# Gated linear attention in a four-layer model: the heads' work as stages between the dense products

## The chip, the cores and the metric

One core of one Trainium2 chip runs the whole program: four layers over 512 tokens of width 1024, batch 1, all in float32. The metric is the device time of one execution in microseconds. Three runs of the kernel before gave a median of 2174.72 us (2171.09 to 2180.26).

## What is computed

Two layers of a first kind, then two of a second; the change touches the first kind alone. Such a layer normalises its input, multiplies it by a wide matrix and splits the result into the inputs of two branches: softmax attention from low-rank q and kv (MLA), and gated linear attention (GLA) with four heads, keys of 64 and values of 128, run forwards and backwards over the sequence. Both branches are gated, joined, projected and added to the residual. The GLA branch in one direction, in chunks of C = 64 tokens:

```python
log_a = log_sigmoid(lr @ w_gate + b_gate) / 16
b   = cumsum(log_a, within the chunk)
ref = b[C // 2 - 1]
A   = tril((q * exp(b - ref)) @ (k * exp(ref - b)).T)
o_intra = A @ v
o_inter = (q * exp(b)) @ state
state   = state * exp(b_last) + (k * exp(b_last - b)).T @ v
o = rmsnorm(o_fwd + o_bwd) * silu(gate)
```

## The kernel before, in words

Every dense product is made of three matmuls on rounded halves (`mm3`, L177 to L179): weights and activations are split into a high part `wh`, `xh` and a rest `wl`, `xl` of type float32r. Weights come as a stream of 128x1024 tiles: `take` (L138 to L142) transfers one on SP's queue into one of two raw buffers, ScalarE rounds it to `wh`, VectorE subtracts for `wl`; there are four buffers of each. `n_out` makes token-major results, four token tiles one after another, each over all eight k; `t_out` makes one feature-major tile of 128x512, from one weight tile.

`layer1` orders a layer so. `ev_kv` normalises and transposes the compressed kv, the rope key and, per token tile, the 32 rows `lrT` of the gates' low-rank input (L601 to L611; transposes use one PSUM bank, `tr`). Then gq and gk (`t_out` four times), gv and the compressed q (`n_out`), the MLA gate `do_ga` (`t_out` four times) and the GLA gate gg (`n_out`). Then `gla(h)` for four heads, then the products of w_uq and w_ukv (`do_qr`, `do_qn`, `do_kn`, `do_vm`), then softmax attention.

One `gla(h)` keeps the forward direction in partitions 0 to 63 and the backward one in 64 to 127. It does: the gate product z from 32 rows in plain float32 (L485); the softplus of it on ScalarE, with Exp and Ln; two scans on VectorE for the sums b; copies of q and k of the head into both halves by DMA on SP's queue (L509, L510); four exponentials (L517) and four products (L518); the scores of both directions into banks 4 and 5 (L531); two predicated copies into masks (L533) and their sum (L535); the transpose of the scaled keys; eight chunk products kv (L543), again into banks 4 and 5; the recurrence of S over the chunks, twelve steps on VectorE (L551, L557); then, per token tile, the own-chunk product (L564) and two products with the states before (L567) into bank 7; normalisation, the gate's factor, and transposes into the layer's output.

What sets the order: the tile framework lays out every engine's queue by a priority that follows program order, and lets a later instruction go first while an earlier one's inputs aren't expected to be ready. `high_priority(offset=n)` moves instructions up by n places. Each engine then runs its queue in order and waits where an input is late:

```python
with tc.high_priority(offset=300):
    for h in range(4):
        gla(h)
```

So the heads come in as soon as their inputs are expected, from the end of `do_ga` on. Weight tiles are moved up by `lead`, 15 or 20 places.

Of the kernel before, what the change touches and what calls it, by code (L numbers as in the profile page):

```python
# [8 lines left out]
F32 = mybir.dt.float32  # L9
# [8 lines left out]
P = 128  # L18
# [19 lines left out]
def shape_consts():  # L38
# [36 lines left out]
    cst1 = np.concatenate([np.broadcast_to(inv1, (P, 32)), scan], 1).astype(f)  # L75
    icst1 = np.concatenate([same & (i <= j), same & (i >= j)], 1).astype(np.int32)
# [12 lines left out]
def body(ctx, tc, a, out, plan, n1=LAYERS, n2=LAYERS, dbg=None):  # L89
# [116 lines left out]
    def n_out(w, xk, c, evac, k_outer=False):  # L206
# [159 lines left out]
    def block1():  # L366
        with ExitStack() as c1:
# [3 lines left out]
            cst1 = b1.tile([P, 32 + SEQ], F32, name="cst1")  # L371
            inv1, scan = cst1[:, 0:32], cst1[:, 32:32 + SEQ]
            icst1 = b1.tile([P, 256], I32, name="icst1")
# [56 lines left out]
            for l in range(n1):  # L430
                xt, xd, pss = layer1(l, xt, xd, CS, SN, scan, icst1, amask, pss)
# [10 lines left out]
    def layer1(l, xt, xd, CS, SN, scan, icst1, amask, pss):  # L442
        lead[0] = 15
        xk = klist(xt)
        with ExitStack() as cl:
# [23 lines left out]
            row, lrT, gate_w = early[:, 0:ROW1], early[0:32, 768:1280], early[:, 1280:1792]  # L469
            nc.sync.dma_start(row, a["row1"][l:l + 1, :].partition_broadcast(P))  # L470
            nc.sync.dma_start(gate_w, a["par1"][l][:, 4:PAR1])
            q_gain, kv_gain, o_gain = row[:, 0:384], row[:, 384:640], row[:, 640:768]
            gqk = pl.tile([P, 4, SEQ], F32, tag="gqk", name="gqk", bufs=1)
# [7 lines left out]
            nc.vector.tensor_scalar(nbias, par[:, 0:4], -1.0, None, ALU.mult)  # L481

            def gla(h):
                z = bank("z")
                nc.tensor.matmul(z, gate_w[0:32, tsl(h)], lrT, start=True, stop=True)  # L485
                bias = par[:, h:h + 1]
                b = gt("wa", 4)
                nc.scalar.activation(b, z, AF.Abs, bias=bias)
                nc.scalar.activation(b, b, AF.Exp, scale=-1.0)
                nc.scalar.activation(b, b, AF.Ln, bias=1.0)  # L490
                la = gt("wa", 4)
                nc.scalar.activation(la, z, AF.Relu, scale=-1.0, bias=nbias[:, h:h + 1])
                nc.vector.tensor_tensor(la, la, b, ALU.add)
# [3 lines left out]
                                             op0=ALU.mult, op1=ALU.add)  # L497
                bv = b.rearrange("p (n c) -> p n c", c=64)
                ref = sml.tile([P, 2, 8], F32, tag="ref", name="ref", bufs=2)
                nc.vector.tensor_copy(ref[F, 0], bv[F, :, 31])  # L500
                nc.vector.tensor_copy(ref[B, 0], bv[B, :, 32])
                nc.vector.tensor_copy(ref[F, 1], bv[F, :, 63])
                nc.vector.tensor_copy(ref[B, 1], bv[B, :, 0])
                dec = sml.tile([P, 8], F32, tag="dec", name="dec", bufs=2)
                nc.scalar.activation(dec, ref[:, 1], AF.Exp, scale=-1 / 16)
                hb = tsl(h % 2, 64)
                q2, k2 = gt("wm", 4), gt("wm", 4)
                for dst, src in ((q2, gq), (k2, gk)):
# [3 lines left out]
                def minus(i):  # L512
                    nc.vector.tensor_tensor(la.rearrange("p (n c) -> p n c", c=64), bv, end(ref[:, i], 64), ALU.subtract)

                def scaled(dst, src, e, s):
                    ex = gt("wa", 4)
                    nc.scalar.activation(ex, e, AF.Exp, scale=s)  # L517
                    nc.vector.tensor_tensor(dst, src, ex, ALU.mult)  # L518
# [878 lines left out]
```

## Time and profile before

| | us |
|---|---|
| median of three runs | 2174.72 |
| lowest, highest | 2171.09, 2180.26 |
| profiled execution, its time | 2182.32 |
| profiled execution, its span | 2180.5 |
| TensorE matmuls busy | 2084.5 |
| VectorE busy | 1271.3 |
| ScalarE busy | 969.2 |
| GpSimd (POOL) busy | 175.7 |

Times in the profile count from the span's start. The mixing stage of layer 0 lies at about 34 to 230 us and that of layer 1 at about 395 to 582; softmax attention follows each. Engines: PE is TensorE's matmuls, PEld its weight loads, DVE is VectorE, ACT is ScalarE. A busy PE is a modelled span of pipelined matmuls, so the distance from one start to the next tells more than a duration.

### The profile page before, as it was taken

Reading aid. Unit: us, or ns where it says so; the run is one execution under the profiler, and the core shown is the slowest. Engines: PE = TensorE matmul, PEld = TensorE weight load, DVE = VectorE, ACT = ScalarE, POOL = GpSimd, SP = SyncE. Lnnn points to the kernel's source line nnn. Section 1 sums busy time; section 2 is a strip of 40 time slices with the busy share of each in tenths; the row PEclk is TensorE's granted clock in tenths of the full one; section 3 lists DMA queues with packets and bytes.
Section 4 is the critical chain, followed back from the end, with each engine's and each line's share of the span. In section 5 each row is a group of like instructions: output and inputs, shape, how many; then the busy total and the mean of one; then the engine's idle time right before and its main releaser. Section 6 shows DMA issues by size and latency. Waiting matters only on the chain.

```text
span 2180.5 us, 28221 instructions
## 1 busy us (share of the span) xinstructions
PE 2084.5 (96%) x10832; PEld 1716.3 (79%) x10832; DVE 1271.3 (58%) x2120; ACT 969.2 (44%) x1819; POOL 175.7 (8%) x305
## 2 busy tenths in 40 slices
PE   7998999998999899999999999999999999999998
PEld 6866887876687788877788888878887778888886
DVE  6278745358855577574466524566757437662464
ACT  4275544355534463336444424446332645442342
POOL 1000000000000211110200000021112011000001
PEclk9999999999999999999999999999999999999999
DMA  5222133332122432121443333243311234333332
GB/s 172 79 73 66 58 108 113 114 109 70 42 97 91 159 113 77 52 64 39 145 152 98 95 96 98 90 129 114 92 54 33 70 116 148 97 98 95 98 98 94
DMA packets 73781, 207.47 MB, mean 95 GB/s; under 512 B 16560, under 2 KB 17584, under 8 KB 73392
## 3 DMA queue, kind: packets, MB, share of 16 engines
q1 hardware_dynamic: 62640, 200.96, 29.5%
q10 hardware_dynamic: 11008, 4.72, 0.9%
q8 instruction: 85, 1.39, 0.3%
q14 instruction: 48, 0.39, 0.1%
HBM read 182.32 MB, written 17.04 MB: 91 GB/s over the span
## 4 chain that ended last, share of the span: by engine, by line
PE 68%; issue 9%; DVE 7%; ACT 7%; DMA 6%; POOL 3%; SPq 0%; POOLq 0%; ACTq 0%; DVEq 0%
PE ps_mm L178 16%; PE ps_mm L179 16%; PE ps_mm L177 16%; DMA wr<-in_w 4%; DVE wl L142 2%; PE ps_o L1188 2%; ACT wh L141 2%; PE ps_tr L270 1%; PE ps_pt L270 1%; POOL rstd L277 1%; PE ps_mo L179 1%; PE ps_mo L177 1%; PE ps_mo L178 1%; PE ps_s L1171 1%; ACT xn L292 1%
## 5 line engine op out<-in xcount | busy, mean ns | idle before, releaser
L142 DVE TENSOR_TENSOR wl<-wr,wh 128x1024 fp32r<-128x1024 f32 (+4 forms) x304 | 360.3, 1188 | 426.3 <-ACT wh L141 422.7
L141 ACT CAST wh<-wr 128x1024 fp32r<-128x1024 f32 (+4 forms) x304 | 309.3, 1019 | 362.5 <-PE ps_mm L179 150.9
L177 PE MATMUL ps_mm<-wh,xh 128*128 128x512 f32 (+2 forms) x736 | 283.8, 387 | 3.3 <-ACT wh L141 3.2
L178 PE MATMUL ps_mm<-wl,xh 128*128 128x512 f32 (+2 forms) x736 | 283.6, 386 | 2.1 <-DVE wl L142 1.8
L179 PE MATMUL ps_mm<-x2h,wl 128*128 128x512 f32 (+1 forms) x768 | 285.5, 372 | 0.0
L177 PE MATMUL ps_mm<-x2h,wh 128*128 128x512 f32 (+1 forms) x768 | 285.4, 372 | 0.0
L178 PE MATMUL ps_mm<-x2l,wh 128*128 128x512 f32 (+1 forms) x768 | 285.4, 372 | 0.0
L179 PE MATMUL ps_mm<-wh,xl 128*128 128x512 f32 (+2 forms) x736 | 282.6, 385 | 0.0
L177 PEld LDWEIGHTS ps_mm<-wh,xh 128*128 128x128 f32 x736 | 140.5, 191 | 30.5 <-ACT wh L141 7.1
L177 PEld LDWEIGHTS ps_mm<-x2h,wh 128*128 128x128 f32 x768 | 144.7, 188 | 25.2
L179 PEld LDWEIGHTS ps_mm<-x2h,wl 128*128 128x128 f32 x768 | 144.7, 188 | 24.9
L178 PEld LDWEIGHTS ps_mm<-x2l,wh 128*128 128x128 f32 x768 | 144.7, 188 | 24.8
L178 PEld LDWEIGHTS ps_mm<-wl,xh 128*128 128x128 f32 x736 | 141.0, 192 | 29.0 <-DVE wl L142 6.0
L179 PEld LDWEIGHTS ps_mm<-wh,xl 128*128 128x128 f32 x736 | 141.0, 192 | 24.9 <-issue 2.2
L1282 DVE SCALAR_TENSOR_TENSOR rt<-ps_mm,par,rt 128x511 f32<-128x511 f32 (+1 forms) x176 | 131.3, 746 | 3.0
L177 PE MATMUL ps_mm<-xh,wh 128*128 128x512 f32 x320 | 127.4, 398 | 0.1
L179 PE MATMUL ps_mm<-xh,wl 128*128 128x512 f32 x320 | 127.4, 398 | 0.0
L178 PE MATMUL ps_mm<-xl,wh 128*128 128x512 f32 x320 | 127.3, 398 | 0.0
L293 POOL TENSOR_SCALAR r2h<-ss 128x1 f32<-128x1 f32 x48 | 18.7, 389 | 961.7 <-ACT th L292 758.8
L178 PE MATMUL ps_mm<-wl,hh 128*128 128x512 f32 x224 | 88.1, 395 | 0.8 <-DVE wl L142 0.8
L177 PE MATMUL ps_mm<-wh,hh 128*128 128x512 f32 x224 | 87.7, 393 | 0.5 <-ACT wh L141 0.4
L179 PE MATMUL ps_mm<-wh,hl 128*128 128x512 f32 x224 | 87.2, 391 | 0.0
(398 smaller groups left out, 3866.7 us busy)
## 6 DMA issues: line engine op xcount, KB each, us to landing
wr<-in_w SPq DMA_DIRECT2D x270, 512.0 KB, 3.6
gain<-in_gain SPq DMA_DIRECT2D x13, 512.0 KB, 6.1
wr<-in_w SPq DMA_DIRECT2D x14, 384.0 KB, 3.2
x<-in_x SPq DMA_DIRECT2D x8, 512.0 KB, 6.0
wm<-gqk SPq DMA_DIRECT2D x32, 128.0 KB, 2.5
xd<-x SPq DMA_DIRECT2D x8, 512.0 KB, 2.6
xs<-xd SPq DMA_DIRECT2D x8, 512.0 KB, 4.0
xs<-xm SPq DMA_DIRECT2D x8, 512.0 KB, 4.5
```

Of the source, the lines that this page charges most:

```text
L141: nc.scalar.copy(hi[:, :n], raw[:, :n])
L142: nc.vector.tensor_tensor(lo[:, :n], raw[:, :n], hi[:, :n].bitcast(F32), ALU.subtract)
L177: nc.tensor.matmul(ps, l[0], r[0], start=start, stop=False)
L178: nc.tensor.matmul(ps, l[0], r[1], start=False, stop=False)
L179: nc.tensor.matmul(ps, l[1], r[0], start=False, stop=stop)
L270: nc.tensor.transpose(ps[:w, tsl(j)], src[:, tsl(j, w)], ident)
L277: nc.gpsimd.tensor_tensor(r2[:, :w], r[:, :w], powm[:, :w], ALU.pow)
L292: nc.scalar.activation(junk[i], halves[i], AF.Square, accum_out=ss[:, i:i + 1])
L293: nc.gpsimd.tensor_scalar(r[:, i:i + 1], ss[:, i:i + 1], 1.0 / D, r[:, 0:1] if i else EPS, ALU.mult, ALU.add)
L1171: nc.tensor.matmul(o_s, q_[own], kl[own, h // 2, :w], start=False, stop=True)
L1188: nc.tensor.matmul(o[:, tsl(h, 64)], p_[:, tsl(i * (qt + 1) + j)], av[:, j, tsl(h, 64)], start=j == 0, stop=j == qt)
L1282: nc.vector.scalar_tensor_tensor(acc[:, j:], ps[:, :SEQ - j], par[:, w0 + 3 * m + 2 - j:w0 + 3 * m + 3 - j], acc[:, j:], ALU.mult, ALU.add)
```

## The change

The gate product takes 96 rows: the low-rank input transposed three times over (high part, high part, rest), against the weights' high part, rest and high part, in float32r. Within a chunk, q and k are scaled once, relative to the chunk's middle; the state is kept relative to the middle of its next chunk, so `dec` spans from middle to middle, the scores' keys serve for the chunk products as well, and q for the past is the scores' q times `dec`, on POOL. The forward scores are multiplied by a mask with 2 on the diagonal of each 64-block; the backward ones are copied over the strictly lower part. A head is cut into eight functions; `n_out` takes a dictionary `then` of what to trace after which token tile. gg now stands before the compressed q. The weighted output overwrites `sgg`. Buffers change: `wm` 4 to 5 (three tiles a head instead of four), `wb` 2 to 1, one `y`, three `gb`, and a tile `lgr` for the gate product's operands; `lrT` and the gate weights leave `early`.

```diff
-    def n_out(w, xk, c, evac, k_outer=False):
+    def n_out(w, xk, c, evac, k_outer=False, then={}):
...
             evac(t, ps)
+            if t in then:
+                then[t]()
...
+            lgr = pl.tile([P, 1024], F32R, name="lgr")
+            lrT, gate_w = lgr[0:96, 0:512], lgr[0:96, 512:1024]
+            nc.scalar.copy(gate_w, gate_raw)
+            nc.vector.tensor_tensor(gate_w[32:64], gate_raw[32:64], gate_w[32:64].bitcast(F32), ALU.subtract)
...
-                nc.tensor.matmul(z, gate_w[0:32, tsl(h)], lrT, start=True, stop=True)
+                nc.tensor.matmul(z, gate_w[:, tsl(h)], lrT, start=True, stop=True)
...
+                for hf, m, e in ((F, 31, 63), (B, 32, 0)):
+                    nc.vector.tensor_copy(ref[hf, 0], bv[hf, :, m])
+                    nc.vector.tensor_tensor(ref[hf, 1], bv[hf, :, e], bv[hf, :, m], ALU.subtract)
+                nc.gpsimd.memset(ref[:, 2], 0.0)
+                nc.gpsimd.tensor_tensor(ref[F, 2, 1:8], ref[F, 0, 1:8], ref[F, 1, 0:7], ALU.add)
+                nc.gpsimd.tensor_tensor(ref[B, 2, 0:7], ref[B, 0, 0:7], ref[B, 1, 1:8], ALU.add)
...
-                minus(0)
-                qi, ki = gt("wm", 4), gt("wm", 4)
-                scaled(qi, q2, la, -1 / 16)
-                scaled(ki, k2, la, 1 / 16)
-                scaled(q2, q2, b, -1 / 16)
-                minus(1)
-                scaled(k2, k2, la, 1 / 16)
+                for x, s in ((ki, 1 / 16), (qi, -1 / 16)):
+                    ex = gt("wa", 4)
+                    nc.scalar.activation(ex, la, AF.Exp, scale=s)
+                    nc.vector.tensor_tensor(x, x, ex, ALU.mult)
+                qe = gt("wm", 5)
+                nc.gpsimd.tensor_tensor(qe.rearrange("p (n c) -> p n c", c=64),
+                                        qi.rearrange("p (n c) -> p n c", c=64), end(dec, 64), ALU.mult)
...
-                for i in range(2):
-                    nc.vector.copy_predicated(amask[i], mid(icst1[:, tsl(i)], NT), v4(sc[i]))
-                A = gt("wb", 2)
-                nc.vector.tensor_tensor(v4(A), amask[0], amask[1], ALU.add)
+                A = amask[h % 2]
+                for u in range(2):
+                    rs = tsl(u, 64)
+                    nc.vector.tensor_tensor(A[rs, :, rs], v4(sf)[rs, :, rs], mid(diag2[rs], NT), ALU.mult)
+                nc.vector.copy_predicated(A, mid(icst1, NT), v4(sb))
...
+            def gla_own(h):
+                gs[h]["o"] = o = bank("og")
+                for t in range(NT):
+                    nc.tensor.matmul(o[:, tsl(t)], gs[h]["A"][:, t], gv[:, t, tsl(h)], start=t == 0, stop=False)
+            def gla_past(h):
+                o, qe, S = (gs[h][n] for n in ("o", "qe", "S"))
+                for n in range(8):
+                    nc.tensor.matmul(o[tsl(n % 2, 64), tsl(n // 2)], qe[:, tsl(n, 64)], S[:, n],
+                                     start=False, stop=n >= 6)
...
-                nc.tensor.transpose(pt[0:32, 384:512], rp[:, 64:96], ident)
+                nc.tensor.transpose(pt[0:96, 384:512], rp[:, 64:160], ident)
...
-                nc.vector.tensor_copy(lrT[:, tsl(t)], pt[0:32, 384:512])
+                nc.vector.tensor_copy(lrT[:, tsl(t)], pt[0:96, 384:512])
+                nc.vector.tensor_tensor(lrT[64:96, tsl(t)], pt[64:96, 384:512], lrT[64:96, tsl(t)].bitcast(F32),
+                                        ALU.subtract)
...
-            with tc.high_priority(offset=300):
-                for h in range(4):
-                    gla(h)
...
+            gla_gate(0)
+            gla_gate(1)
+            do_gqk(0)
+            gla_scale(0)
+            gla_gate(2)
+            do_gqk(1)
+            gla_scale(1)
+            n_out(take_n("w_in", l, rng(6), range(KT)), xk, 512,
+                  lambda t, ps: nc.scalar.copy(gv[:, t], ps), then={1: lambda: gla_scores(0), 2: lambda: gla_gate(3)})
+            n_out(take_n("w_in", l, rng(9), range(KT)), xk, 512, ev_gg, then={
+                0: lambda: (gla_state(0), gla_scale(2)), 1: lambda: gla_own(0),
+                2: lambda: (gla_scores(1), gla_past(0)), 3: lambda: gla_state(1)})
+            n_out(take_n("w_in", l, rng(0), range(KT)), xk, 384, ev_q, then={
+                0: lambda: (gla_norm(0), gla_scale(3)), 1: lambda: gla_own(1), 2: lambda: gla_scores(2),
+                3: lambda: gla_past(1)})
+            do_ga(0)
+            gla_state(2)
+            gla_norm(1)
+            do_ga(1)
+            gla_own(2)
+            gla_scores(3)
+            do_ga(2)
+            gla_past(2)
+            gla_state(3)
+            do_ga(3)
+            gla_norm(2)
...
+                         range(3)), cq, 256, ev_qr, then={1: lambda: gla_own(3), 3: lambda: gla_past(3)})
+            do_qn(0)
+            gla_norm(3)
+            do_qn(1)
+            gla_out(0)
             do_kn()
+            for h in (1, 2, 3):
+                gla_out(h)
             do_vm()
```

## Rows read from the trace of the kernel before

**Rows 1.** The page, engine totals: busy us (share of the span), instructions.
```profile
PE 2084.5 (96%) x10832; PEld 1716.3 (79%) x10832; DVE 1271.3 (58%) x2120; ACT 969.2 (44%) x1819; POOL 175.7 (8%) x305
```

**Rows 2.** Stretches: from:to, length, busy us of PE, PEld, DVE, ACT, POOL, granted clock, DMA.
```profile
34.00:110.00 76.00, 72.25 (x344) 61.46 (x343) 28.35 (x63) 26.21 (x51) 6.15 (x14) 0.98 0.30 97
110.00:230.00 120.00, 107.06 (x573) 78.00 (x573) 95.27 (x176) 71.94 (x150) 7.12 (x14) 0.91 0.26 72
170.00:230.00 60.00, 50.92 (x316) 37.51 (x315) 48.87 (x98) 30.02 (x80) 5.06 (x10) 0.91 0.28 77
460.00:582.00 122.00, 107.30 (x596) 79.08 (x595) 97.42 (x180) 72.88 (x151) 7.68 (x15) 0.96 0.26 78
520.00:582.00 62.00, 52.87 (x333) 39.11 (x332) 51.05 (x101) 31.65 (x83) 5.24 (x10) 0.94 0.25 75
```

**Rows 3.** Timeline of PE: start us, us, instruction [idle before <-releaser].
```profile
138.19 0.39 PE L178 MATMUL ps_mm<-wl,xh 128*128 128x512 f32 x1
138.42 0.39 PE L179 MATMUL ps_mm<-wh,xl 128*128 128x512 f32 x1
141.16 0.44 PE L567 MATMUL ps_og<-S,wm 128*64 128x128 f32 x4 [2.35 <-issue]
...
145.84 0.63 PE L178 MATMUL ps_mm<-wl,xh 128*128 128x512 f32 x1
146.27 0.63 PE L179 MATMUL ps_mm<-wh,xl 128*128 128x512 f32 x1
```

**Rows 4.** Groups of DVE in 110:230: count | busy us, mean ns | idle before.
```profile
L557 DVE SCALAR_TENSOR_TENSOR S<-S,dec,ps_kv 64x128 f32<-64x128 f32 x24 | 8.5, 354 | 0.8
L551 DVE SCALAR_TENSOR_TENSOR S<-S,dec,ps_kv 64x128 f32<-64x128 f32 x24 | 8.1, 339 | 0.8
```

**Rows 5.** Waits of PE in 110:232: us in total, times, longest.
```profile
PE ps_kv L543 <- ACT wb L539: 2.0, 1, 2.0
PE ps_mm L177 <- ACT th L658: 1.7, 1, 1.7
```

**Rows 6.** Timeline of PE around one gate product.
```profile
129.16 1.12 PE L485 MATMUL ps_z<-early 32*128 32x512 f32 x2 [0.15 <-ACT wa L492]
130.21 0.66 PE L270 MATMUL ps_ks<-ident,wm 128*128 128x128 f32 x4
130.62 0.48 PE L179 MATMUL ps_mm<-xh,wl 128*128 128x512 f32 x1
```

**Rows 7.** Timeline of PE in one head's output product, at full clock.
```profile
184.12 0.44 PE L567 MATMUL ps_og<-S,wm 128*64 128x128 f32 x4 [0.30 <-issue]
184.49 0.49 PE L564 MATMUL ps_og<-gv,wb 128*128 128x128 f32 x2
...
185.28 0.49 PE L564 MATMUL ps_og<-gv,wb 128*128 128x128 f32 x2
```

**Rows 8.** Groups of ACT and DVE in 110:230 (one layer).
```profile
L517 ACT ACTIVATE wa<-wa 128x512 f32<-128x512 f32 x16 | 9.8, 630 | 3.8 <-DVE wm L518 3.1 <-DVE wa L513 0.5
L518 DVE TENSOR_TENSOR wm<-wm,wa 128x512 f32<-128x512 f32 x16 | 10.8, 688 | 3.7 <-PE ps_og L567 3.5
```

**Rows 9.** Timeline of POOL and of DVE at 844 us, in the second block.
```profile
844.40 2.53 POOL L1063 TENSOR_TENSOR dt<-A,cst 128x512 f32<-128x512 f32 x2
844.46 1.24 DVE L1014 TENSOR_SCALAR cq<-rstd 128x4 f32<-128x4 f32 x1
```

**Rows 10.** Timeline of PE and of DVE, transposes of kv.
```profile
401.13 0.41 PE L270 MATMUL ps_tr<-ident,th 128*128 128x128 f32 x2 [0.92 <-DVE early L611]
40.66 0.28 DVE L611 COPY early<-ps_tr 32x128 f32<-32x128 f32 x1
```

**Rows 11.** Timeline of PE where the compressed q follows gv, layers 0 and 1.
```profile
86.53 0.62 PE L177 MATMUL ps_mm<-wh,xh 128*128 128x384 f32 x2 [1.66 <-ACT wh L141]
...
445.23 0.44 PE L178 MATMUL ps_mm<-wl,xh 128*128 128x384 f32 x1 [0.21 <-DVE wl L142]
```

**Rows 12.** Waits of SP's queue, whole span: us in total, times, longest.
```profile
SPq L509 <- PE ps_sb L531: 12.6, 4, 5.6
```

More of the change, by code (lines that the diff above doesn't have):

```diff
@@ L509, in gla @@
+                for dst, src in ((qi, gq), (ki, gk)):
                     nc.sync.dma_start(dst[F], src[h // 2][hb])
                     nc.sync.dma_start(dst[B], src[h // 2][hb])
[L512 to L515 removed]
+                la = gt("wa", 4)
+                nc.vector.tensor_tensor(la.rearrange("p (n c) -> p n c", c=64), bv, end(ref[:, 0], 64), ALU.subtract)
@@ L561, in gla @@
-                with tc.high_priority(offset=-20):
-                    o = bank("og")
-                    for t in range(NT):
-                        nc.tensor.matmul(o[:, tsl(t)], A[:, tsl(t)], gv[:, t, tsl(h)], start=True, stop=False)
-                        for u in range(2):
-                            n = 2 * t + u
-                            nc.tensor.matmul(o[tsl(u, 64), tsl(t)], q2[:, tsl(n, 64)], S[:, n], start=False, stop=True)
-                    y = gt("wb", 2)
-                    ss = sml.tile([P, 4], F32, tag="ss4", name="ss4")
-                    for t in range(NT):
-                        nc.scalar.activation(y[:, tsl(t)], o[:, tsl(t)], AF.Square, accum_out=ss[:, t:t + 1])
-                    r = rstd(ss, 4, 1.0 / P)
-                    for t in range(NT):
-                        nc.scalar.activation(y[:, tsl(t)], o[:, tsl(t)], AF.Copy, scale=r[:, t:t + 1])
-                    nc.vector.tensor_tensor(v4(y), v4(y), sgg[:, :, tsl(h)], ALU.mult)
-                    ps = flip(y, role="og")
-                    split(ps, yt[0][1][:, h], yt[1][1][:, h])
+                nc.scalar.copy(S[F, 1], kv[0][F, tsl(0)])
@@ new lines, in gla_state @@
+                nc.scalar.copy(S[B, 6], kv[1][B, tsl(3)])
+                for n in range(1, 7):
+                    m = 7 - n
+                    nc.vector.scalar_tensor_tensor(S[F, n + 1], S[F, n], dec[F, n:n + 1],
+                                                   kv[n % 2][F, tsl(n // 2)], ALU.mult, ALU.add)
+                    nc.vector.scalar_tensor_tensor(S[B, m - 1], S[B, m], dec[B, m:m + 1],
+                                                   kv[m % 2][B, tsl(m // 2)], ALU.mult, ALU.add)
@@ new lines, in gla_norm @@
+            def gla_norm(h):
+                o = gs[h]["o"]
+                y = gt("y", 1)
+                ss = sml.tile([P, 4], F32, tag="ss4", name="ss4")
+                for t in range(NT):
+                    nc.scalar.activation(y[:, tsl(t)], o[:, tsl(t)], AF.Square, accum_out=ss[:, t:t + 1])
+                r = rstd(ss, 4, 1.0 / P)
+                for t in range(NT):
+                    nc.scalar.activation(y[:, tsl(t)], o[:, tsl(t)], AF.Copy, scale=r[:, t:t + 1])
+                nc.vector.tensor_tensor(sgg[:, :, tsl(h)], v4(y), sgg[:, :, tsl(h)], ALU.mult)
@@ L579, in layer1, with gla_out @@
+            def gla_out(h):
+                ps = bank("og")
+                for t in range(NT):
+                    nc.tensor.transpose(ps[:, tsl(t)], sgg[:, t, tsl(h)], ident)
+                split(ps, yt[0][1][:, h], yt[1][1][:, h])
             ckh = pc.tile([P, 2, SEQ], F32R, name="ckh")
```

130 lines of the change are left out of this document (57 added, 73 removed).

## The prediction

> **What bounds the kernel now.** I read the page's engine totals first. TensorE's matmuls are busy for 96% of the span [rows 1], so time is won only where TensorE idles, runs below full clock, or issues less. Next I cut the span into stretches, each layer's mixing stage apart [rows 2]. Its dense first part (34 to 110 us) is nearly full on TensorE while VectorE works 28.35 of 76 us. The part with the heads is different: in layer 0 (110 to 230 us) TensorE is busy 107.06 of 120 us at a mean granted clock of 0.91, and in layer 1 (460 to 582 us) 107.30 of 122 at 0.96. Idle time is 12.9 + 14.7 = 27.6 us. Clock lost, (1 - 0.91) x 120 + (1 - 0.96) x 122, is 15.7 us at most, since part of the slow time is itself idle. Together 43.3 us: the whole pool of waiting that the change can touch.
>
> Then the order of time on TensorE shows what one such wait looks like [rows 3]. Dense matmuls follow each other every 0.23 us; then head 0's output product, hoisted 300 places up, arrives before its states exist and TensorE idles 2.35 us. Afterwards a 512-column matmul takes 0.43 us from start to start: the clock was at 1.2 instead of 2.4 GHz. What it waits for is twelve recurrence steps on VectorE, 0.34 and 0.35 us each [rows 4], about 4.2 us in a row. The wait view of the same stage lists other waits of this kind, on a PSUM copy and on an eviction queued behind head work on ScalarE [rows 5]. So four heads run as chains at the end of the stage, over the short w_uq and w_ukv products, where they cover badly.
>
> **The change, part by part.**
>
> *Order.* The four heads become stages between the dense products. Between a head's state and the product that reads it now stand two dense tiles (heads 0 and 2), four of cq (head 1), or one and the four small ones of qr (head 3); a 512-wide tile is 24 matmuls x 0.23 = 5.5 us. The recurrence's 4.2 us, plus one weight split ahead of it on VectorE, fits in one or two. The second half of the stage (qr, qn, kn, vm) keeps head 3's past product, two normalisations and all output transposes. There the idle time was 60 - 50.92 = 9.1 us and 62 - 52.87 = 9.1 us [rows 2]; I keep half, 9.1 us over both layers. Of the clock loss I keep a quarter, 3.9 us, since half-rate stretches follow the waits. Kept 13.0 of 43.3, so gained 30.3 us. The ends: everything kept (0) and everything gone (43.3). I take a value nearer the upper end because the first-half stages get tens of microseconds of dense cover that the rows show VectorE and ScalarE idle in.
>
> *Gate product.* Before, one head's product is two records of a plain fp32 matmul over 32 rows, 1.05 us from its start to the next instruction [rows 6]. After, it is one fp32r matmul over 96 rows and 512 columns, a form the trace has not got; the nearest rows are the dense fp32r matmuls over 128 rows, 0.23 us from start to start [rows 3]. Saved 0.82 x 8 heads = 6.6 us; the ends are 0.23 and twice that, so 4.7 to 6.6. Making the 96 rows costs one ScalarE copy and one VectorE subtract per layer, under the 22 us of gq/gk products, and one more small VectorE subtract per token tile (below).
>
> *Output product.* Before, own-chunk and past products alternate: 0.79 us per token tile from own product to own product [rows 7], 3.15 us per head. After, eight own instructions run together, then sixteen past ones. No row shows either run alone. Past: four instructions took 0.37 us between switches [rows 7], so sixteen take 1.5. Own: a pair took 0.79 - 0.37 = 0.42 us with its two switches, so four pairs at most 1.7; at the transposes' pace, four in 0.41 us [rows 6], 0.8. Between 2.3 and 3.2 us a head; I take 2.35, near the lower end because the switches leave. Saved 0.8 x 8 = 6.4 us, ends 0 and 6.8.
>
> *Fewer exponentials and masks.* Two of four exponentials and their two products go (0.63 us on ScalarE, 0.69 on VectorE each [rows 8]), also one subtraction of the reference, one predicated copy and the sum of the two masks; two half-size products with the diagonal mask come. This lightens VectorE and ScalarE by some 2.6 and 1.3 us a head. On the bounding engine it is worth nothing by itself: I cost it at nothing, as part of why waits shrink.
>
> *Product moved to POOL.* The scaled query for the past product is now a POOL multiplication. Nearest row: two 128x512 products there took 2.53 us, so 1.27 each [rows 9]. It is needed only at the past product, a tile or more later. On POOL's queue the clears of S, which wait for the previous head's past product, and the rstd steps of cq stand behind or ahead of it; cq is wanted only at the end of the dense part. Cost 0; without that cover up to 8 x 1.27 = 10.2 us.
>
> *Transposes of kv.* TensorE already waits 0.92 us for the copy of the low-rank rows to free the transposes' bank [rows 10]. The new subtract after it, like that copy, takes 0.28 us; up to 8 x 0.28 = 2.2 us, at least 0. I take about half, 1.2 us lost, since only tiles that wait for the bank pay.
>
> *Weights.* Two token-major products in a row need four new weight tiles at once from four buffers. Before, one such border per layer cost 1.66 us in layer 0 and 0.21 in layer 1 [rows 11]. Now there are two (gv to gg, gg to cq). One more per layer at the mean, 0.94: 1.9 us; ends 0 and, every border at 1.66, 4.8.
>
> *Transfers.* The q and k copies, four DMA instructions a head, stay on SP's queue; three tiles per head now share five buffers, so the k copy of head 2 waits for head 0's past product and head 3's for head 1's. Weight transfers stand behind them. I cost this at nothing, as the copies are laid where the buffer is expected free; the price if that fails is rival C.
>
> Sum: 30.3 + 6.6 + 6.4 - 1.2 - 1.9 = 40.2 us. The profiled execution took 2182.3 us (span 2180.5, 1.8 around it), 7.6 above the median of the three runs; it would take 2142.1. Against the median, 2174.7 - 40.2 = **2134.5, so 2135 us**.
>
> **The rivals.**
>
> *B, the waits stay.* The new places are only priorities: the heads' work may again land where its inputs come late. Then only work leaves: 6.6 + 6.4 - 3.1 = 9.9 us, 2165. For it: the queues have been laid out with waits in them before [rows 3]. Against: the hoist by 300 places, which put the products there, is gone.
>
> *C, SP's queue is held, and it gets slower.* Head 2's k copy, issued at gg's first tile, waits for a buffer that head 0's past product frees two tiles later (11.0 us); head 3's, at cq's first tile, waits three tiles of cq, estimated by their width at 3/4 of 5.5 us each, 12.4 us. All weights behind stand still and TensorE runs dry: 2 x 23.4 = 46.8 us, plus some ten matmuls at 0.2 us more [rows 3] after each of four holds, 8. Net 54.8 - 40.2 = 14.6 us slower, 2189. It decides once the holds cost TensorE over 40 us. For it: q copies already held SP for a PE release four times, 12.6 us in total [rows 12]. Against: the longest such hold was 5.6 us, and six converted or raw tiles stand ready.
>
> *D, all waits go.* 43.3 instead of 30.3: 53.2 us, 2121.5. For it: VectorE's free time in the dense part [rows 2]. Against: qr's rope chain in the late half stays.
>
> *E, POOL's product holds VectorE.* A VectorE operation on four columns took 1.24 us because it began under a POOL product [rows 9]; another blocked op could be the weight split on which TensorE waits. At 8 x 1.27 us the gain falls by 10.2 to 30.0: 2145. For it: that row. Against: the heads now stand where weight splits have slack. The Trainium skill, "SBUF — State Buffer", section "Who interferes with whom", says that a VectorE instruction with two SBUF inputs contends with a GpSimd instruction that reads SBUF, and that whichever comes second blocks for the whole instruction. The row agrees for a one-input operation; by that rule every weight split could be hit, which is this rival at full price.
>
> **How the numbers follow.** Chances: forecast 0.60 (its own range 2122 to 2150, from the bounds of waits, output product and weights), B 0.12, C 0.07, D 0.13, E 0.08. Half a percent, 10.9 us, is about what a measurement of this kernel can tell from no change. The forecast, D and E are faster by more than that: 0.81. B is within it: 0.12. C is slower: 0.07. The range that holds 8 in 10 takes in the forecast, D with a margin of 3 us below, for its other terms at their best ends, E, and the near side of B: 2118 to 2164.
>
> **What would show each step.** Right: idle TensorE time in each layer's mixing stage under about 6 us, clock near 1.0; gate records single and near 0.39 us long, next start 0.23 later; own and past products each in one run; VectorE busier before 110 us and less so after. Wrong: past products still preceded by 1 us waits (B); q and k copies on SP waiting for PE with weights behind them, TensorE idle on wh (C); weight splits above 2 us (E).

## The result, and the profile after

The changed kernel takes **2142.14 us** in the median of four runs (2137.47 to 2145.0). The kernel before took 2176.14 (four runs, 2171.09 to 2180.26). The ratio is 0.984, with a 95% interval from 0.981 to 0.987: 28 to 40 us saved, against 40.2 forecast; the two medians differ by 34.0. The profiled execution took 2143.14 us where the one of before took 2182.32, so 39.2 less. All balances below are made within these two. The one of before is the slowest of the 49 on record, 6.2 us above its median and at a granted clock of 0.987 where 44 others have a median of 0.991, so some 5 of the 39.2 us belong to that execution and not to the change.

First the engine totals of the profile's page after, which answer to [rows 1]:

```profile
PE 2059.3 (96%) x10824; PEld 1709.0 (80%) x10824; DVE 1261.0 (59%) x2106; ACT 959.2 (45%) x1805; POOL 195.5 (9%) x337
```

TensorE's share is unchanged at 96%, of a span 39.1 us shorter. Next the windows of after, at three of the stretches of [rows 2] (columns as there):

```profile
34.00:110.00 76.00, 67.85 (x306) 52.88 (x305) 52.40 (x112) 47.66 (x79) 11.04 (x20) 0.96 0.34 97
110.00:230.00 120.00, 117.61 (x725) 99.67 (x723) 85.82 (x163) 60.82 (x148) 11.57 (x26) 1.00 0.25 76
460.00:582.00 122.00, 118.92 (x747) 102.20 (x745) 94.61 (x189) 65.84 (x158) 9.65 (x21) 1.00 0.23 71
```

VectorE now works 52.40 us before 110 us, where it worked 28.35. Behind 110 us TensorE idles 2.4 us and, in layer 1, 3.1 us, at full clock, where 12.9 and 14.7 us were idle. Before 110 us the opposite happened: idle time rose from 3.75 to 8.15 us and the clock fell from 0.98 to 0.96.

Fixed times hold other work after than before, so the balance needs stretches that hold the same work: from the last first-projection product to the last product of full attention's scores, in each layer. First the kernel before, then after:

```profile
34.26:257.79 223.53, 206.84 (x1074) 162.55 (x1073) 150.31 (x300) 117.52 (x245) 13.27 (x28) 0.95 0.25 74
392.91:609.40 216.49, 200.16 (x1074) 158.34 (x1073) 148.48 (x292) 115.34 (x242) 11.76 (x26) 0.98 0.26 77
```

```profile
35.44:238.01 202.57, 192.02 (x1070) 158.26 (x1069) 144.47 (x293) 112.11 (x238) 22.61 (x46) 0.98 0.27 82
373.79:574.52 200.73, 190.66 (x1070) 157.01 (x1069) 143.18 (x285) 110.88 (x234) 21.77 (x41) 0.99 0.28 83
```

The two stages together shrank from 440.0 to 403.3 us: 36.7 of the 39.2. Idle TensorE time fell from 33.0 to 20.6 (12.4 us). Clock lost, (1 - clock) x length, comes to 15.5 us before and 6.1 after from the two decimals of these lines. It is read more closely from windows cut to the stretches at half clock; here is one of before, behind the wait of [rows 3], and one of after:

```profile
142.00:148.83 6.83, 6.83 (x32) 4.47 (x33) 4.10 (x6) 3.15 (x13) 2.06 (x4) 0.50 0.21 60
```

```profile
39.08:42.49 3.41, 3.41 (x10) 2.65 (x9) 2.39 (x9) 2.97 (x7) 1.12 (x2) 0.50 0.22 79
```

TensorE is busy in them, so next to nothing is counted twice, as idle time and as lost clock. In the two stages they add up to 23.9 + 10.2 us before and 6.8 + 3.4 us after. Half of that is lost: 17.1 us before, 5.1 after, so 12.0 us came back. The rest, 36.7 - 12.4 - 12.0 = 12.3 us, is TensorE work that is no longer there. The 2.5 us outside the two stages were not taken apart.

What is left of waiting, by the wait view of TensorE after, layer 0 (34 to 212 us) and then layer 1 (374 to 548 us). Columns: what waits and for what, us in total, times, longest.

```profile
PE ps_mm L180 <- DVE wl L144: 2.9, 4, 1.6
PE ps_z L497 <- ACT wa L503: 2.4, 1, 2.4
PE ps_mm L179 <- DVE sga L364: 1.2, 1, 1.2
PE ps_tr L274 <- DVE th L613: 1.1, 1, 1.1
PE ps_mm L179 <- DVE rp L358: 0.9, 1, 0.9
PE ps_tr L274 <- DVE th L358: 0.9, 1, 0.9
PE ps_mm L179 <- ACT wh L143: 0.6, 1, 0.6
...
PE ps_mm L180 <- DVE wl L144: 5.0, 5, 2.3
PE ps_tr L274 <- DVE lgr L640: 1.2, 2, 0.6
...
PE ps_z L497 <- ACT wa L503: 1.1, 1, 1.1
```

No line of the head's own products (scores, states, own, past) is left. In the same stages before, the past products alone had waited 4.2 and 5.8 us. The profile puts those down to issue, but the product of [rows 3] starts at 141.16 us, 0.11 behind the end of VectorE's last recurrence step. The largest line is now the weights' low half: with the high half 9.1 us over both layers, against 2.1 in the stages before.

Three pieces of TensorE's order of time after: head 0's past product, its own product, and the gate product of head 1 (columns: start, us, engine, line, what).

```profile
118.03 0.66 PE L274 MATMUL ps_ks<-ident,wm 128*128 128x128 f32 x4
118.61 1.09 PE L587 MATMUL ps_og<-S,wm 128*64 128x128 f32 x16
119.64 0.50 PE L179 MATMUL ps_mm<-wh,xh 128*128 128x512 f32 x1
...
110.47 1.05 PE L582 MATMUL ps_og<-gv,amask 128*128 128x128 f32 x8
111.27 0.48 PE L179 MATMUL ps_mm<-wh,xh 128*128 128x512 f32 x1
...
61.72 0.40 PE L497 MATMUL ps_z<-lgr 96*128 96x512 f32 x1
61.95 0.40 PE L181 MATMUL ps_mm<-xh,wl 128*128 128x512 f32 x1
```

The past product follows its predecessor without a wait, sixteen instructions in one run of 1.03 us to the next start; the own product is one run of 0.80. The gate product is one record of 0.40 us with the next start 0.23 later. Over both layers the eight heads differ: 0.81 to 1.05 us for own products, 1.03 for past products (1.45 for head 3's, which transposes cut in two), 0.23 to 0.34 for gates.

### The profile page after: what moved, and what is told of

It reads as the page before. It is cut to its first block, busy times and chain, and to the rows that moved or that the text cites. A ratio compares the mean times of both kernels' runs of the same rounds, so it can differ in the third digit from the quotient of the medians.

```text
span 2141.4 us, 28239 instructions
## 1 busy us (share of the span) xinstructions
PE 2059.3 (96%) x10824; PEld 1709.0 (80%) x10824; DVE 1261.0 (59%) x2106; ACT 959.2 (45%) x1805; POOL 195.5 (9%) x337
## 3 DMA queue, kind: packets, MB, share of 16 engines
q1 hardware_dynamic: 62576, 200.80, 30.3%
## 4 chain that ended last, share of the span: by engine, by line
PE 76%; DVE 7%; ACT 6%; DMA 5%; issue 4%; POOL 3%; POOLq 0%; ACTq 0%; SPq 0%; DVEq 0%
PE ps_mm L180 18%; PE ps_mm L181 18%; PE ps_mm L179 18%; DMA wr<-in_w 4%; DVE wl L144 2%; PE ps_tr L274 2%; PE ps_o L1237 2%; ACT wh L143 2%; PE ps_pt L274 1%; PE ps_mo L181 1%; PE ps_mo L179 1%; PE ps_mo L180 1%; PE ps_s L1220 1%; POOL r2h L297 1%; ACT xn L296 1%
```

## The experiments

Twelve variants with four or five runs each, hoist with twelve. "Against after" is the median minus 2142.14; the kernel before, run beside them, had medians of 2174.26 to 2176.66. The runs of one variant lie up to 8 us apart, so differences below some 5 us are not told apart.

| variant of the changed kernel | median (lowest to highest), us | ratio to before, 95% interval | against after |
|---|---|---|---|
| gate32 | 2153.87 (2148.9 to 2157.13) | 0.990 [0.9886, 0.9913] | +11.7 |
| alternate | 2148.61 (2148.36 to 2155.27) | 0.9888 [0.9874, 0.9902] | +6.5 |
| hoist | 2172.97 (2169.95 to 2177.68) | 0.9988 [0.9978, 0.9998] | +30.8 |
| heavy | 2147.64 (2144.93 to 2149.46) | 0.9875 [0.9862, 0.9888] | +5.5 |
| gates | 2145.82 (2144.32 to 2148.5) | 0.9859 [0.9837, 0.9881] | +3.7 |
| border | 2151.44 (2148.93 to 2151.85) | 0.9879 [0.986, 0.9897] | +9.3 |
| bank6 | 2144.32 (2142.61 to 2147.97) | 0.9852 [0.983, 0.9874] | +2.2 |
| qe_vec | 2145.26 (2141.52 to 2148.14) | 0.9853 [0.983, 0.9875] | +3.1 |
| spread | 2145.98 (2145.61 to 2147.81) | 0.9865 [0.9846, 0.9885] | +3.8 |
| lead30 | 2141.9 (2141.09 to 2145.86) | 0.9848 [0.9828, 0.9869] | -0.2 |
| wm6 | 2141.39 (2140.85 to 2144.69) | 0.9848 [0.9828, 0.9868] | -0.8 |
| both | 2139.54 (2137.91 to 2142.47) | 0.9845 [0.9831, 0.9858] | -2.6 |

### First set: the parts of the change, one undone at a time

Theory W: the gain is TensorE work that left plus waits that the new order removes. Rival L: the waits went because VectorE and ScalarE have less to do for each head, in whatever order.

**hoist: the old order with the new arithmetic.**

```diff
+            with tc.high_priority(offset=300):
+                for h in range(4):
+                    gla_gate(h)
+                    gla_scale(h)
+                    gla_scores(h)
+                    gla_state(h)
+                    with tc.high_priority(offset=-20):
+                        gla_own(h)
+                        gla_past(h)
+                        gla_norm(h)
+                        gla_out(h)
```

> The changed kernel's arithmetic (96-row gate product, two exponentials, one mask copy, POOL product, own and past each in a run) with the heads traced as four whole chains after gg, hoisted 300 places, and the dense products in the order of before. Theory W: the waits come back; slower than the changed kernel by 34 - 12 = 22 us, about 2164, with 1.5 us waits and more before the past products and a clock of 0.91 to 0.96 in the mixing stages. Rival L: most of the gain stays, at most 8 us slower, 2150.

It took 30.8 us back, some 9 more than the theory and nearly four times what the rival allows. TensorE's largest waits in its layer 0 (35 to 254 us), and the windows of its two stages:

```profile
PE ps_ks L274 <- DVE wm L535: 5.0, 3, 2.1
PE ps_mm L179 <- ACT th L676: 4.2, 3, 3.3
PE ps_og L587 <- DVE S L575: 2.7, 2, 2.0
...
```

```profile
35.01:253.97 218.96, 199.38 (x1070) 163.52 (x1069) 144.08 (x293) 112.16 (x238) 21.39 (x46) 0.97 0.25 76
389.57:603.66 214.09, 200.47 (x1070) 162.96 (x1069) 141.66 (x284) 110.07 (x234) 18.87 (x41) 0.97 0.26 77
```

The stages idle 33.2 us, as much as before (33.0), though the arithmetic is the new one: the waits of the heads are back, on the scaled keys, the states, and qr's eviction queued behind heads on ScalarE. Against after, the two stages are 433.1 - 403.3 = 29.8 us longer: 12.6 us of idle time, 8.5 of clock (27.3 us at half clock against 10.2), and 8.7 of TensorE time that is no wait. The first two are the 22 us that theory W named. The rest are longer steps, some of them of the chunk products, which are busy for 7.0 us in layer 0 against 5.9 after and 4.6 before; why was not taken apart. The waits for weights, 9.1 us after, are 2.6 here.

So **without the order 3 of the 34 us are left**: the cheaper arithmetic in the old order is worth 3 us of its 13. The 31 are not a share beside those of other parts, for undoing the order, the gate product and the runs of the output product one at a time gives 30.8 + 11.7 + 6.5 = 49.0. The changed kernel's numbers of buffers stay in hoist; whether they add to its waits was not tested.

**gate32: the gate product in plain fp32.**

```diff
...
-            lrT, gate_w = lgr[0:96, 0:512], lgr[0:96, 512:1024]
+            lrT, gate_w = lgr[0:32, 0:512], gate_raw[0:32]
...
-                nc.tensor.transpose(pt[0:96, 384:512], rp[:, 64:160], ident)
+                nc.tensor.transpose(pt[0:32, 384:512], rp[:, 64:96], ident)
```

> The changed kernel with the gate product back in plain fp32 on 32 rows (two records per head), and the transposed rows back to 32 without the extra subtract; the order by stages stays. Theory W (the gain is waits that go through the order, plus 13 us of shorter TensorE work): slower than the changed kernel by 6.6 - 1.2 = 5.4 us, so about 2148 where the changed kernel takes 2142; gate records again two per head and 1.05 us to the next start. Rival L (the gain comes from lighter work on VectorE and ScalarE): no difference beyond 2 us. Both: the mixing stage of a layer grows by 2 to 4 us.

11.7 us, twice the expectation, though its five runs lie between 2148.9 and 2157.13 and the difference is known to some 5 us. The product itself costs what was reckoned (1.05 us to the next start, against 0.23 to 0.34). The rest shows in the order of time of the profiled execution, the longest of the five: behind the gates a weight is later than before, and the clock falls to half.

```profile
76.76 0.50 PE L179 MATMUL ps_mm<-wh,xh 128*128 128x512 f32 x1 [3.10 <-ACT wh L143]
...
77.34 0.44 PE L181 MATMUL ps_mm<-wh,xl 128*128 128x512 f32 x1
77.58 0.63 PE L179 MATMUL ps_mm<-wh,xh 128*128 128x512 f32 x1
78.01 0.63 PE L180 MATMUL ps_mm<-wl,xh 128*128 128x512 f32 x1
```

In this execution the two stages are 14.3 us longer than after: 3.2 of idle time, 5.1 of clock and 6.0 of TensorE work, near the 5.4 that were expected. Changed is the time of ScalarE's steps relative to TensorE; that the longer products alone shift it, and not the other copies, was not taken apart.

**alternate: own and past products in turns.**

```diff
-                for t in range(NT):
-                    nc.tensor.matmul(o[:, tsl(t)], gs[h]["A"][:, t], gv[:, t, tsl(h)], start=t == 0, stop=False)
...
+                for t in range(NT):
+                    nc.tensor.matmul(o[:, tsl(t)], gs[h]["A"][:, t], gv[:, t, tsl(h)], start=True, stop=False)
+                    for n in (2 * t, 2 * t + 1):
+                        nc.tensor.matmul(o[tsl(n % 2, 64), tsl(t)], qe[:, tsl(n, 64)], S[:, n], start=False, stop=True)
```

> The changed kernel with own-chunk and past products alternating per token tile again, the own product moved to the past product's place. Theory W: slower by 6.4 us (0.8 per head), 2148; own and past together again take about 3.15 us per head from first start to the next dense start. If the two runs apart are no cheaper than the alternation, it is the same as the changed kernel, and that term of the sum was wrong.

6.5 us, as forecast. In its trace the turns are back at 0.79 us per token tile, 3.05 us a head, and the two stages hold 6.3 us more TensorE work.

**heavy: VectorE's and ScalarE's old load as idle work.**

```diff
+                la = gt("wa", 4)
+                nc.vector.tensor_tensor(la.rearrange("p (n c) -> p n c", c=64), bv, end(ref[:, 1], 64), ALU.subtract)
+                for x in (ki, qi):
+                    ex = gt("wa", 4)
+                    nc.scalar.activation(ex, la, AF.Exp, scale=-1 / 16)
+                    nc.vector.tensor_tensor(ex, x, ex, ALU.mult)
...
+                junk = gt("wa", 4)
+                nc.vector.tensor_copy(junk, sb)
+                nc.vector.tensor_tensor(junk, junk, A.rearrange("p t c -> p (t c)"), ALU.add)
```

> The changed kernel with idle work put back per head on the engines that the change relieved: one more reference subtraction, two more exponentials, two more products, one more PSUM copy and one more sum (3.4 us of VectorE and 1.3 us of ScalarE a head). Theory W: it lies under dense cover, at most 4 us slower, 2142 to 2146. Rival L: it gives back the gain, 15 to 30 us slower, 2157 or more.

5.5 us: just above theory W's bound, far from L's 15, and hardly clear of no change. It put 23.5 us on VectorE in the two stages (311.1 busy against 287.6), so most of such work does not reach the end. The lighter head steps are at most a help to the order, not the source of its gain.

### Second and third set: can the waits that are left be taken?

The waits left stand behind one picture. VectorE after, in order of time, around the gates of heads 0 and 1:

```profile
65.89 0.69 DVE L504 TENSOR_TENSOR wa<-wa 128x512 f32<-128x512 f32 x1 [4.89 <-ACT wa L501]
66.61 1.22 DVE L506 TENSOR_TENSOR_SCAN gb<-cst,wa 64x512 f32<-64x512 f32 x1
...
70.34 0.69 DVE L504 TENSOR_TENSOR wa<-wa 128x512 f32<-128x512 f32 x1 [1.26 <-ACT wa L501]
...
74.91 1.23 DVE L144 TENSOR_TENSOR wl<-wr,wh 128x1024 fp32r<-128x1024 f32 x1
```

The weight split comes behind both gates, though ScalarE had rounded its tile by 71.73. It ends at 76.14, and TensorE starts on it at 76.19 after 0.84 us of idleness; in layer 1 the same tile costs 2.26 us. At the border of gv and gg the block is head 3's scans and scaling steps of other heads, and the wait 1.65 us.

**gates: ScalarE's steps grouped, the bank freed early.**

```diff
-                nc.scalar.activation(sp, sp, AF.Exp, scale=-1.0)
-                nc.scalar.activation(sp, sp, AF.Ln, bias=1.0)
...
+                    nc.scalar.activation(la, z, AF.Relu, scale=-1.0, bias=nbias[:, h:h + 1])
+                for h, sp, la in st:
+                    nc.scalar.activation(sp, sp, AF.Exp, scale=-1.0)
+                for h, sp, la in st:
+                    nc.scalar.activation(sp, sp, AF.Ln, bias=1.0)
...
-            gla_gate(0)
-            gla_gate(1)
+            gla_gate(0, 1)
```

> The changed kernel with the gates' ScalarE steps in another order: Relu directly behind Abs, so that the gate product's PSUM bank is free before the exponential, and the gates of heads 0 and 1 taken together, both exponentials and then both logarithms. In the changed kernel's trace ScalarE loads its function table five times, 1.28 us each, between 61 and 73 us of layer 0, because exponential and logarithm alternate over heads 0 and 1, and the gate product of head 2 then waits 2.44 us in layer 0 and 1.13 us in layer 1 for ScalarE's Relu, with a half-clock stretch of some 3 us behind the first. Theory T (these loads and the late Relu make that wait): both waits go, and about 1.5 us of lost clock, so 3.6 + 1.5 = 5 us faster than the changed kernel, 3 to 7. Rival (TensorE is early there and waits for the next late thing, a weight tile): within 1.5 us of the changed kernel, and a weight wait near 76 us that grows by what the gate wait gave.

The rival's picture. The gate's wait is gone from both layers, and two table loads with it; TensorE reaches the weight tile earlier and waits there, and the waits for weights grow from 9.1 to 13.1 us over both layers. VectorE and then TensorE of this variant:

```profile
74.41 1.22 DVE L144 TENSOR_TENSOR wl<-wr,wh 128x1024 fp32r<-128x1024 f32 x1
```

```profile
75.69 0.53 PE L180 MATMUL ps_mm<-wl,xh 128*128 128x512 f32 x1 [4.25 <-DVE wl L144]
76.02 0.62 PE L181 MATMUL ps_mm<-wh,xl 128*128 128x512 f32 x1
```

The split ends 0.5 us earlier, so TensorE gains 0.5 us there out of the 2.44 taken away, and the one long wait is followed by half clock (0.42 us from 76.02 to the next start). The median, 3.7 us above the changed kernel's, is not told apart from it.

**spread: one gate at a time between the dense products.**

```diff
...
             gla_gate(0)
-            gla_gate(1)
             do_gqk(0)
             gla_scale(0)
-            gla_gate(2)
+            gla_gate(1)
             do_gqk(1)
             gla_scale(1)
+            gla_gate(2)
```

> The changed kernel with the head's gates spread out: gate 0 before the first gq/gk product, gate 1 behind it, gate 2 behind the second (before: gates 0 and 1 ahead of the first, gate 2 behind it), and in each the Relu directly behind the Abs. In the changed kernel's trace the gates of heads 0 and 1 stand together on VectorE (sum, two scans, reference steps: from 65.9 to 74.9 us of layer 0), and the weight split on which TensorE waits comes behind them. Theory Q (what is left of waiting in the first half is weight splits and bank releases queued behind head steps on VectorE and ScalarE, and goes when the head steps come in smaller blocks): the waits for the gate's bank (2.44 and 1.13 us) and for the split (0.84 and 2.26 us) go with their half-clock stretches, 6.7 us and up to 3 more, so 5 to 9 us faster than the changed kernel. Rival (the blocks only move: head 1's scores or head 2's gate come late in gv or gg): within 2 us of the changed kernel or up to 4 us slower.

The Relu directly behind the Abs, as in gates, is in this variant too. The rival again, at its slower end. In layer 0 the gate's wait is still 1.3 us and the weight waits grew from 3.5 to 7.3.

**border: a feature-major product between token-major ones.**

```diff
                   lambda t, ps: nc.scalar.copy(gv[:, t], ps), then={1: lambda: gla_scores(0), 2: lambda: gla_gate(3)})
+            do_ga(0)
+            gla_state(0)
+            gla_scale(2)
             n_out(take_n("w_in", l, rng(9), range(KT)), xk, 512, ev_gg, then={
...
+            do_ga(1)
+            gla_own(1)
             n_out(take_n("w_in", l, rng(0), range(KT)), xk, 384, ev_q, then={
```

> The changed kernel with a feature-major product of the output gate (ga 0) put between gv and gg and another (ga 1) between gg and cq, so that no two token-major products with four new weight tiles each follow each other; the head stages stand after the same number of dense tiles as before. In the changed kernel's trace each layer has three weight waits at the border of gv and gg, 0.17 + 0.55 + 1.65 = 2.4 us in layer 0 and the same in layer 1. Theory (borders cost by their four tiles at once): these waits go, 4.7 us faster than the changed kernel, 2 to 7. Rival (the weight splits are late because they queue behind head steps on VectorE, wherever the border is): waits of the same size at other places, within 2 us of the changed kernel or up to 5 us slower, as two more activations per tile come in between.

9.3 us slower, beyond the rival's 5. The border moved and its wait with it: now the recurrence's twelve steps stand ahead of a split on VectorE.

```profile
104.02 0.33 DVE L573 SCALAR_TENSOR_TENSOR S<-S,dec,ps_kv 64x128 f32<-64x128 f32 x1
...
108.17 0.35 DVE L575 SCALAR_TENSOR_TENSOR S<-S,dec,ps_kv 64x128 f32<-64x128 f32 x1
108.55 1.23 DVE L144 TENSOR_TENSOR wl<-wr,wh 128x1024 fp32r<-128x1024 f32 x1
```

TensorE waited 1.63 us for it, at 109.83. A new wait before scores, 1.9 us in layer 0 (head 3's) and 2.2 in layer 1, which the profile puts down to issue, came on top. By the order of time it is for the bank: these scores go into the banks from which head 2's recurrence still reads. Its last step but one ends at 163.50 us and the scores start at 163.60; in layer 1, 502.35 and 502.45.

**bank6: a fourth bank for the late half.**

```diff
             lead[0] = 20
+            banks["mm"] = (0, 1, 2, 6)
```

> The changed kernel with a fourth PSUM bank for the dense products of the stage's late half (the bank of the keys' transposes, free after head 3's scores). In the changed kernel's trace the first product of qr waits 1.20 us in each layer for VectorE's last product of the output gate, which holds the bank. Theory (the bank is the wait): 2.4 us faster than the changed kernel, 1 to 4. Rival (the rope chain of qr behind it is what is late): within 1 us of the changed kernel, with the wait moved to the transposes of qr.

The rival's wait: the first product of qr no longer waits, but its rope chain does. Layer 0 after, then of this variant:

```profile
181.92 0.39 PE L179 MATMUL ps_mm<-wh,cq 128*128 128x256 f32 x1 [1.20 <-DVE sga L364]
```

```profile
181.59 0.63 PE L274 MATMUL ps_tr<-ident,th 128*64 128x128 f32 x4 [1.46 <-DVE th L358]
```

The medians cannot tell it from the changed kernel.

**qe_vec: the scaled query's product on VectorE.**

```diff
-                nc.gpsimd.tensor_tensor(qe.rearrange("p (n c) -> p n c", c=64),
+                nc.vector.tensor_tensor(qe.rearrange("p (n c) -> p n c", c=64),
                                         qi.rearrange("p (n c) -> p n c", c=64), end(dec, 64), ALU.mult)
```

> The changed kernel with the scaled query's product (128x512, one a head) on VectorE instead of POOL. Theory (the product on POOL costs nothing, forecast term 0): the same time within 2 us, or up to 3 us slower, as VectorE gets 8 x 0.69 = 5.5 us more work in front of weight splits. Rival E (POOL's product holds VectorE, part of the waits that are left): 3 to 10 us faster.

3.1 us above the changed kernel, not told apart from it; nothing for rival E.

**lead30, wm6, both: weights asked for earlier, one more buffer for queries and keys.**

```diff
-        lead[0] = 15
+        lead[0] = 30
...
-                qi, ki = gt("wm", 5), gt("wm", 5)
+                qi, ki = gt("wm", 6), gt("wm", 6)
...
-                qe = gt("wm", 5)
+                qe = gt("wm", 6)
```

> The changed kernel with weights asked for 30 places ahead instead of 15 in the dense part of the stage. On VectorE one weight split then stands ahead of head 0's subtraction of the reference and some of the small steps (about 1 us earlier) in layer 0, and two do in layer 1 (up to 2.6 us earlier); the rest of the order stays. Theory Q (those splits queue behind head steps): the waits of 0.84 and 2.26 us shrink by 0.8 and some 2, with part of layer 1's half-clock stretch of 3.3 us, so 3 to 5 us faster than the changed kernel. Rival (the head steps, now later, are themselves waited for): within 1 us.

> The changed kernel with six buffers instead of five for the scaled queries and keys, so that the q and k copies on SP's queue wait less for a TensorE release. Rival C's mechanism stands in the changed kernel's trace (q/k copies held SP's queue for the scores four times, 51.4 us, longest 13.9), but no weight transfer seems to be due behind them. Theory (those holds cost nothing): within 2 us of the changed kernel. Rival C in part (weights behind the copies come late, and the weight waits at the border of gv and gg, 2.4 us a layer, are from there): 3 to 5 us faster.

> The changed kernel with the two edits together that came out fastest alone by their profiled spans: weights asked for 30 places ahead (2139.2 us) and six buffers for scaled queries and keys (2139.1, against 2141.4 of the changed kernel). If the two gains are real and each takes away its own wait (the split behind head steps in layer 1; the q and k copies), they add: some 4 us under the changed kernel, a median near 2138. If they are chance or take away the same wait: within 2 us of the changed kernel, 2140 to 2144.

lead30 took the weights' low-half waits in layer 1 from 5.0 to 3.7 us, less than half of what theory Q wanted, and the median stood within the rival's 1 us. wm6 is within its 2 us too, so the held queue costs nothing that shows. Together they leave 5.9 of the 9.1 us of weight waits, and the median is 2.6 us under the changed kernel's; the ratios to the kernel before, 0.9845 and 0.9843, have overlapping intervals, so the two are not told apart. No variant beats the changed kernel by more than its measurement tells.

## Why the prediction was right, and where its terms were off

- **Direction, time, range.** 2135 forecast, 2142.14 measured, inside 2118 to 2164 and inside the forecast's own 2122 to 2150. The medians differ by 34.0 us where 40.2 were forecast; the two profiled executions by 39.2. That closeness is in part luck, twice. The pool's 15.7 us of lost clock were read at the profiled execution's granted clock of 0.987; at the median of 0.991 there is less to win back, which is argued from the clocks and was not traced. And within the balance two misses of opposite sign cancel, below.
- **Order, 30.3 less 1.2 and 1.9, so 27.2 net.** Measured 12.4 + 12.0 = 24.4 in the stages, where 15.4 of idle time and 11.8 of clock were forecast. The mechanism is shown by hoist: with the chains back, the idle time is back. The late half kept less than thought: two waits a layer, 1.2 + 0.9 us, 4.2 in all where 9.1 were kept. The first half kept more, the weights above all. The sign of being right that I had named, under about 6 us of idle time in each layer's stage, did not come: it is 10.5 and 10.1.
- **Weights, -1.9: the step that failed.** I counted one more border of two token-major products and priced it from [rows 11]. The border gv to gg did cost 0.17 + 0.55 + 1.65 = 2.4 us a layer. But the weight waits rose from 2.1 to 9.1 us, 7.0 lost, because the head steps now run among the dense tiles and sit ahead of splits on VectorE, borders or not; in hoist, with the same steps behind the wide dense tiles, they are 2.6. I had named VectorE's free time as cover, and missed that its queue is in order: free time on average is not a free place in front of a split.
- **Transposes of kv, -1.2.** The waits on the low-rank copy itself did not grow, 1.6 us in the two stages before and 1.5 after. A new one of 0.95 us came in layer 0 behind the rope and the copies, with seven matmuls at half clock behind it, about 0.2 us each: some 2.4 us. In gate32, which has not got these copies, that wait is missing and the granted clock from 36 to 44 us is 1.00, where it is 0.79 after.
- **Gate product, 6.6.** Right by rows: over the eight gates 0.29 us to the next start in the mean, against 1.05 [rows 6], so 6.1. Undoing it costs 11.7, known to some 5 us.
- **Output product, 6.4.** About right. A head's runs take 2.04 us in the mean, a little less than the 2.35 that I took. But I read the time before too high as well: 3.15 us is four times one tile's turn, while the heads at full clock took 2.87 to 3.06, as the first own product had gone ahead by itself. So some 7.5 us over eight heads; undoing it costs 6.5. Gate and output product together are 13.6 by rows, 13.0 in the sum; 12.3 show as work gone.
- **Fewer exponentials and masks, 0.** Perhaps too low: heavy says up to 5.5, an upper bound since its idle work loads VectorE by 12.3 us more than the kernel before had (311.1 against 298.8), and itself hardly clear of no change.
- **POOL's product, 0; rival E.** Right in price: the longest weight split is 1.23 us. On POOL the product took 1.37 us where it began 0.21 us after a VectorE instruction with two SBUF inputs, and 1.04 where no such one ran beside it:

```profile
77.48 1.37 POOL L537 TENSOR_TENSOR wm<-wm,dec 128x512 f32<-128x512 f32 x1 [0.68 <-POOL ref L522]
...
143.06 1.04 POOL L537 TENSOR_TENSOR wm<-wm,dec 128x512 f32<-128x512 f32 x1 [0.56 <-PE ps_ks L274]
```

  At 77.48 POOL came second and POOL was the slower one. Rival E's mechanism is in the trace once, in layer 1, where VectorE came second: the subtraction that takes 0.68 us at 77.27 took 1.53 under a POOL product.

```profile
408.67 1.91 POOL L537 TENSOR_TENSOR wm<-wm,dec 128x512 f32<-128x512 f32 x1 [0.68 <-POOL ref L522]
409.60 1.53 DVE L531 TENSOR_TENSOR wa<-gb,ref 128x512 f32<-128x512 f32 x1
```

  The rule of the Trainium skill that the prediction weighed ("SBUF — State Buffer", section "Who interferes with whom") agrees with the direction in both places. By the same section of the Trainium skill, a VectorE instruction with at most one SBUF input contends only in a two-port mode. Whether the one of [rows 9] ran in such a mode no row shows; the subtraction, with two inputs, is the case that the rule names. No weight split began under one of the eight POOL products, so what that would cost was not measured.
- **Transfers, 0; rival C.** Its mechanism is there, its price is not. SP's queue, layer 0 (34 to 212 us) after:

```profile
SPq L140 <- DVE wl L144: 98.3, 22, 14.7
SPq L528 <- PE ps_sb L547: 25.8, 2, 13.9
```

  The q and k copies held the queue twice for scores, up to 13.9 us, longer than I had priced; for the past products that I had named they held it 0.4 us. But the weight transfers wait for a buffer 98.3 us in the same stretch, so most would have waited anyway, and a sixth buffer (wm6) changed nothing that could be told.
- **Rival B** is excluded by the past products without waits, **D** by 20.6 us of idleness left.

## What to carry to other kernels

When a serial stage is spread under dense products, list for each in-order engine what then stands ahead of the operand preparation of those products: the waits do not vanish, they move to the weights. Price the order by running the new arithmetic in the old order (here 3 of the 34 us were left). A small wait taken away alone gives little if the next late thing is on another engine's queue; here eight variants, of one such step or two, gained nothing that could be measured.

## What the runs showed of the hardware

- Alternating exponential and logarithm over two heads cost ScalarE five function-table loads in 12 us. ScalarE after, in order of time:

```profile
61.41 1.28 ACT L500 ACT_TABLE_LOAD   x1
63.93 1.28 ACT L501 ACT_TABLE_LOAD   x1
65.87 1.28 ACT L500 ACT_TABLE_LOAD   x1
68.39 1.28 ACT L501 ACT_TABLE_LOAD   x1
71.75 1.28 ACT L524 ACT_TABLE_LOAD   x1
```

  The Trainium skill, "ScalarE: Activation LUTs", section "Table sets: the hidden batching unit", says that a logarithm and then an exponential share one set and need one load. This trace differs: each change of the two is a load of 1.28 us, and the trace decides. Grouping them took two of the five away, and no time that could be measured.
- The past products, sixteen instructions of a 128x64 with a 128x128 tile that accumulate, run in 1.03 us when nothing stands between them, 0.064 each; in turns with the own products, four took 0.37 us up to the next own product [rows 7], 0.093 each.
- Like waits were not followed by the same clock. After, two waits of 1.14 and 0.95 us end at 36.91 and 38.29 us of layer 0; seven matmuls at half clock follow (0.43 us from start to start), and the granted clock from 36 to 44 us is 0.79. In bank6 two waits of 1.14 and 0.94 us end at 36.00 and 37.38, and it is 1.00 in the same window. After, a wait of 1.65 us that ends at 101.74 is not followed by half clock either (0.23 to 0.24 from start to start behind it).
